# Newton's steps of two inverse roots, column by column or over all columns at once

## The chip, the core and the metric

The kernel runs on one core of a Trainium2 chip. A core has five engines that work side by side, each through its own list of instructions in order: TensorE (PE in the profile, with its weight loads as PEld), VectorE (DVE), ScalarE (ACT), GpSimd (POOL) and SyncE (SP), which here only issues transfers. The engines wait for one another by semaphores. The metric is the time of one execution on the device in microseconds (us). Lower is better.

## The reference, cut to what matters

The reference is one layer of a sequence encoder over 1024 tokens of 1024 channels. It normalises x, projects it, runs two mixers (a state-space scan, S5, and Hyena, which convolves with long filters), merges them and projects again. Two inverse square roots matter here.

The first belongs to Hyena's filters. Each of 2048 filters (2 orders, 1024 channels) has its own two-sided response k of 2048 steps, scaled to unit length:

```
k = k * lax.rsqrt(jnp.sum(k * k, axis=0, keepdims=True) + HY_EPS)
```

The second belongs to the RMSNorm of x, one number for each of 1024 tokens:

```
y = xf * lax.rsqrt(jnp.mean(xf * xf, axis=-1, keepdims=True) + RMS_EPS)
```

## The kernel before, in words

The first 260 us build the filters' spectra. The work is cut into eight units of 256 filters (order o, quarter cq). A unit has two parts. `filter_time` runs over eight tiles of 128 time steps: PE multiplies a small network's output into the tile (`g`, L333 and L334), ACT makes the decay (`e`, L336), DVE multiplies both (`e`, L338, one input from PSUM), ACT squares (`sq`, L342), DVE or POOL forms sums and differences (`so`, `ss`, `sd`, L349 and L350), ACT and DVE split those of the odd tiles in two parts (`sh`, `sl`, L109 and L113), and POOL adds up the squares (`acc`, L357, two SBUF inputs of 128x512). `filter_freq` is the cosine and sine transform of the unit before: PE multiplies (`po` L404, `pe` L414), DVE joins the halves (`ke` L425 and L426, `ko` L429 and L430).

Between them stands `filter_norm`: PE sums the squares over the partitions (`q`, L371), DVE adds the epsilon (`qs`, L375), calls `rsqrt` on a tile of 128x2, and forms from its result a correction that PE transposes (L381, L383) and DVE adds to one row of the sums (`ss`, L386). So `rsqrt` is called eight times with two columns (result `nrm`). `conv_weights` later reads all of `nrm` (L569 to L572).

In the same stretch `norm_in` prepares x piece by piece between the tiles of the units: four loads, sixteen squares on ACT, then on DVE the sum (`ssq`, L460, L462) and one call of `rsqrt` with eight columns (result `rs`), then ACT scales x by `rs` (`xr`, L468), PE transposes it (`xt`, L475), and ACT and DVE split it (`xh` L479, `xl` L480). The sums over x are taken while the second unit runs and the root while the third does.

`rsqrt` (L115) starts from a bit trick (L119), scales v by -0.5 (L121), and takes three Newton steps y = y (1.5 + v y y). A step is written column by column: L125 forms z = (y v) y for one column, with v as a scalar per partition, and L126 forms y = (z + 1.5) y. With two columns that is 12 instructions, with eight columns 48, each on a tile of 128x1.

The order of each engine's list is set when the program is built, by a planner that simulates the timeline (`schedule_with_timeline_sim=True`) and picks among the instructions that are ready by priority. `filter_norm` has raised priority (L285). `issue_after` (L288, L291) ties the other parts to steps of `filter_time`. The planner may put other instructions between the steps of one `rsqrt`.

After the units come the projections (`pps`, L556), S5, the Hyena convolutions and the output, mostly on PE.

Of the kernel before, what the change touches and what calls it, by code (L numbers as in the profile page):

```python
# [12 lines left out]
ALU = mybir.AluOpType  # L13
# [87 lines left out]
class Trunk:  # L101
# [13 lines left out]
    def rsqrt(self, pool, out, v, n):  # L115

        V = self.nc.vector
        h = pool.tile([128, n], F, name="rsq_h", tag="rsq_h")
        V.tensor_scalar(out=out.bitcast(I32), in0=v.bitcast(I32), scalar1=-0.5, scalar2=float(0x5F3759DF),  # L119
                        op0=ALU.mult, op1=ALU.add)  # L120
        V.tensor_scalar(out=v, in0=v, scalar1=-0.5, scalar2=None, op0=ALU.mult)  # L121
        for _ in range(3):
            for c in range(n):
                y, z = out[:, c:c + 1], h[:, c:c + 1]
                V.scalar_tensor_tensor(out=z, in0=y, scalar=v[:, c:c + 1], in1=y, op0=ALU.mult, op1=ALU.mult)  # L125
                V.scalar_tensor_tensor(out=y, in0=z, scalar=1.5, in1=y, op0=ALU.add, op1=ALU.mult)  # L126

    def reduce_2pi(self, out, x, k):
        nc = self.nc
# [1410 lines left out]
```

## Time and profile before

| | us |
|---|---|
| median of 3 runs | 1416.13 (1413.56 to 1418.54) |
| the profiled execution | 1413.96 |
| its span in the trace | 1412.2 |
| PE busy | 1346.7 (95%) |
| DVE busy | 1014.1 (72%), 1934 instructions |
| ACT busy | 515.1 (36%) |
| POOL busy | 416.6 (29%) |
| chain that ended last | PE 72%, DVE 18% of the span |

Times in a profile are microseconds from the start of the span. Busy time is summed over the instructions of an engine. A busy PE is not PE at its peak, since its records are pipelined. PEclk is the clock that was granted to TensorE as a share of 2.4 GHz. The chain that ended last is followed back from the last instruction: at each step to what released it, or to the instruction before it on its engine.

### The profile page before, as it was taken

To read this page: it belongs to the slowest core of one execution; us is meant where nothing else is said; L and a number is where in the kernel's file an instruction comes from. 1 tells how busy PE (TensorE), PEld (TensorE's weight loads), DVE (VectorE), ACT (ScalarE), POOL (GpSimd) and SP (SyncE) were. 2 spreads that over 40 slices of the span, in tenths; PEclk is the share of its full clock that TensorE was granted. 3 is DMA by queue.
4 is the path that set the end of the run, shared out by engine and by line. 5 is a ranking of instruction groups with operands and counts; after the bars stand their busy time and mean duration, and the time that the engine had idled before them with its cause. 6 is when DMAs were issued, how large, how long until landed. Compare 5 with 4: busy or idle time off the path is not lost.

```text
span 1412.2 us, 19536 instructions
## 1 busy us (share of the span) xinstructions
PE 1346.7 (95%) x7219; PEld 1135.9 (80%) x7219; DVE 1014.1 (72%) x1934; ACT 515.1 (36%) x737; POOL 416.6 (29%) x343
## 2 busy tenths in 40 slices
PE   5888899999999999999999997999999999999997
PEld 3777798888888887788788885998888889878886
DVE  7999997699599887414479997663899836843632
ACT  5576664222332333333322222443222234422422
POOL 3766675000000000223112213743013223322322
PEclk9999999999999999999999998999999999999999
DMA  8222224865695554566985588769888988755431
GB/s 278 94 78 75 77 100 146 200 173 137 164 301 132 124 124 103 134 173 155 307 244 173 172 241 264 216 179 315 258 268 268 292 247 245 220 161 134 139 112 64
DMA packets 188556, 257.24 MB, mean 182 GB/s; under 512 B 23069, under 2 KB 144153, under 8 KB 185724
## 3 DMA queue, kind: packets, MB, share of 16 engines
q1 hardware_dynamic: 148492, 151.32, 34.0%
q0 software_dynamic: 12608, 43.79, 15.6%
q10 hardware_dynamic: 27360, 60.88, 12.0%
q8 instruction: 57, 0.93, 0.3%
q14 instruction: 39, 0.32, 0.1%
HBM read 147.49 MB, written 76.82 MB: 159 GB/s over the span
## 4 chain that ended last, share of the span: by engine, by line
PE 72%; DVE 18%; DMA 5%; issue 3%; ACT 1%; POOL 1%; SPq 0%; ACTq 0%; DVEq 0%; POOLq 0%
PE pps L556 43%; PE ops L1441 6%; PE iv L643 5%; PE po L404 4%; PE fwo L695 3%; DMA zc<-c_zc_lo_d 2%; PE pe L414 2%; PE pps L536 2%; DVE rsq_h L125 2%; DVE e L338 1%; PE fwe L695 1%; DMA d_y<-x 1%; DVE st L1274 1%; PE zt L680 1%; DVE st L1272 1%
## 5 line engine op out<-in xcount | busy, mean ns | idle before, releaser
L512 POOL DMA_DIRECT2D wlo<-wraw x76 | 66.3, 872 | 673.3 <-ACT wlo L511 530.2
L556 PE MATMUL pps<-xh,whi 128*128 128x512 f32 x848 | 214.2, 400 | 3.2 <-DVE cv L581 3.2
L556 PE MATMUL pps<-xl,whi 128*128 128x512 f32 x848 | 212.3, 397 | 0.0
L556 PE MATMUL pps<-xh,wlo 128*128 128x512 f32 x848 | 210.2, 396 | 0.0
L556 PEld LDWEIGHTS pps<-xh,whi 128*128 128x128 f32 x848 | 158.0, 189 | 39.5 <-ACT wlo L511 3.6
L556 PEld LDWEIGHTS pps<-xh,wlo 128*128 128x128 f32 x848 | 157.9, 188 | 36.8
L556 PEld LDWEIGHTS pps<-xl,whi 128*128 128x128 f32 x848 | 157.3, 188 | 36.3 <-issue 0.2
L510 ACT CAST whi<-wraw 128x1024 fp32r<-128x1024 f32 (+1 forms) x76 | 74.7, 982 | 285.7 <-PE pps L556 254.9
L404 PE MATMUL po<-sh,fo 128*128 128x256 f32 x512 | 101.1, 292 | 6.0 <-DVE sh L111 5.1
L643 PE MATMUL iv<-ic,y 128*128 128x256 f32 (+1 forms) x752 | 97.2, 287 | 5.5 <-POOL y L113 3.1
L643 PEld LDWEIGHTS iv<-ic,y 128*128 128x128 f32 x752 | 95.4, 194 | 8.1 <-POOL y L113 4.0
L404 PEld LDWEIGHTS po<-sh,fo 128*128 128x128 f32 x512 | 84.0, 197 | 8.3 <-DVE sh L111 6.1
L357 POOL TENSOR_TENSOR acc<-acc,sq 128x512 f32<-128x512 f32 x56 | 75.9, 1356 | 24.5 <-ACT sq L342 23.0
L511 ACT ACTIVATE wlo<-whi 128x1024 fp32r<-128x1024 f32 (+1 forms) x76 | 74.9, 985 | 20.7 <-PE pps L556 20.6
L113 DVE TENSOR_TENSOR y<-yraw,y 128x512 fp32r<-128x512 f32 x60 | 55.0, 938 | 28.2 <-ACT y L109 28.2
L404 PE MATMUL po<-sl,fo 128*128 128x256 f32 x256 | 74.2, 290 | 1.0 <-DVE sl L113 1.0
L579 DVE SCALAR_TENSOR_TENSOR cv<-pps,cw,cv 128x1023 f32<-128x1023 f32 x24 | 30.7, 1281 | 59.5 <-ACT cv L578 59.5
L109 ACT CAST y<-yraw 128x512 fp32r<-128x512 f32 x64 | 39.0, 619 | 55.9 <-DMA yraw<-d_y 27.4
L404 PEld LDWEIGHTS po<-sl,fo 128*128 128x128 f32 x256 | 50.4, 197 | 2.2 <-DVE sl L113 1.3
L578 ACT ACTIVATE cv<-pps,cb,cw 128x1024 f32<-128x1024 f32 x24 | 29.0, 1208 | 62.1 <-PE pps L556 43.9
L333 PE MATMUL g<-w3h,ha 128*128 128x512 f32 x64 | 33.3, 520 | 18.6 <-DVE e L338 17.6
L695 PE MATMUL fwo<-z,zc 128*128 128x256 f32 x384 | 49.9, 283 | 0.0
(447 smaller groups left out, 2788.7 us busy)
## 6 DMA issues: line engine op xcount, KB each, us to landing
wlo<-wraw POOLq DMA_DIRECT2D x64, 512.0 KB, 5.7
wraw<-w_in SPq DMA_DIRECT2D x56, 512.0 KB, 5.2
kspec<-ko SPq DMA_DIRECT2D x32, 512.0 KB, 3.6
kt<-kspec SPq DMA_DIRECT2D x32, 512.0 KB, 5.1
yraw<-d_y SPq DMA_DIRECT2D x64, 256.0 KB, 5.3
d_y<-x ACTq DMA_DIRECT2D x28, 512.0 KB, 5.5
d_m<-cv ACTq DMA_DIRECT2D x16, 512.0 KB, 2.6
d_z<-z ACTq DMA_DIRECT2D x8, 1024.0 KB, 5.5
```

The costliest lines, as they stand in the source:

```text
L109: nc.scalar.copy(out=hi, in_=src)
L113: e.tensor_tensor(out=lo, in0=src, in1=hi, op=ALU.subtract)
L333: nc.tensor.matmul(out=ps, lhsT=ha[:, tsl], rhs=w3h, start=True, stop=False)
L357: nc.gpsimd.tensor_tensor(out=acc, in0=acc, in1=sq, op=ALU.add)
L404: nc.tensor.matmul(out=po[:, part], lhsT=fo[a][:, 12 * (jj % 2) + b], rhs=sd[4 + i][d][:, part], start=n == 0 and part == 0, stop=n == 11 ...
L510: nc.scalar.copy(out=hi, in_=raw)
L511: nc.scalar.activation(out=lo, in_=hi, func=AF.Copy, scale=-1.0)
L512: nc.gpsimd.dma_start(out=lo, in_=raw, accum_op=ALU.add)
L556: self.summed = nc.tensor.matmul(out=ps[:, hf * 512:hf * 512 + 512], lhsT=w[:, kc], rhs=part(x, kc, hf), start=a == 0 and p == 0 and kc == ...
L643: self.rotated = nc.tensor.matmul(out=dst, lhsT=lhsT, rhs=self.ic[b, j][:, cols], start=first, stop=last)
L695: nc.tensor.matmul(out=out, lhsT=zc[a][:, b], rhs=z[:, :, d, zi], start=start and n == 0, stop=stop and n == 3 * len(prods) - 1)
L1441: nc.tensor.matmul(out=pss[cs.start][:, 0:cs.stop - cs.start], lhsT=m[:, kc, ts], rhs=w[kc][:, cs], start=kc == 0 and p == 0, stop=kc == 7 ...
```

## The change

Each Newton step is now three instructions over the whole tile, whatever the number of columns: h = y y, h = h v, y = (h + 1.5) y. A call has nine instructions in its steps, on 128x2 in `filter_norm` and on 128x8 in `norm_in`. The bit trick and the scaling ahead of them stay.

```diff
         for _ in range(3):
-            for c in range(n):
-                y, z = out[:, c:c + 1], h[:, c:c + 1]
-                V.scalar_tensor_tensor(out=z, in0=y, scalar=v[:, c:c + 1], in1=y, op0=ALU.mult, op1=ALU.mult)
-                V.scalar_tensor_tensor(out=y, in0=z, scalar=1.5, in1=y, op0=ALU.add, op1=ALU.mult)
+            V.tensor_tensor(out=h, in0=out, in1=out, op=ALU.mult)
+            V.tensor_tensor(out=h, in0=h, in1=v, op=ALU.mult)
+            V.scalar_tensor_tensor(out=out, in0=h, scalar=1.5, in1=out, op0=ALU.add, op1=ALU.mult)
```

## Rows read from the trace of the kernel before

**Rows 1.** The page, chain that ended last, shares of the span by engine.

```profile
PE 72%; DVE 18%; DMA 5%; issue 3%; ACT 1%; POOL 1%; SPq 0%; ACTq 0%; DVEq 0%; POOLq 0%
```

**Rows 2.** Busy time by stretch, one filter unit each: stretch, length, busy, PEclk, DMA.

```profile
45.40:70.50 25.10, 21.47 (x119) 18.23 (x120) 24.65 (x50) 15.91 (x27) 19.30 (x19) 0.93 0.31 111
70.50:97.80 27.30, 23.80 (x147) 20.80 (x147) 25.62 (x49) 23.13 (x56) 18.90 (x20) 0.97 0.25 86
97.80:132.90 35.10, 29.41 (x171) 25.70 (x171) 34.33 (x104) 17.84 (x32) 19.79 (x21) 0.87 0.24 88
132.90:160.70 27.80, 25.77 (x160) 23.03 (x160) 27.25 (x52) 19.77 (x36) 18.48 (x20) 0.94 0.23 80
160.70:185.90 25.20, 22.20 (x144) 19.76 (x144) 24.06 (x51) 16.83 (x30) 20.78 (x20) 1.00 0.21 72
185.90:213.10 27.20, 27.14 (x184) 24.76 (x184) 27.10 (x55) 19.09 (x32) 20.45 (x23) 1.00 0.25 96
213.10:237.50 24.40, 23.01 (x152) 20.59 (x151) 22.87 (x47) 10.71 (x19) 17.50 (x18) 1.00 0.22 87
237.50:260.00 22.50, 22.50 (x148) 20.76 (x148) 10.51 (x47) 5.28 (x6) 1.78 (x2) 1.00 0.90 236
```

**Rows 3.** The same view, finer, inside the third unit.

```profile
115.00:122.00 7.00, 6.98 (x22) 5.67 (x23) 7.00 (x21) 6.43 (x12) 4.07 (x5) 0.62 0.19 71
```

**Rows 4.** The chain in order of time, third unit: start, us on the chain, what.

```profile
112.54 0.60 DVE rsq_h L125
113.14 1.23 DVE rs L126 x2
114.37 0.61 DVE e L338
...
116.24 3.41 PE pe L414 x8
...
120.08 1.90 PE pe L414 x8
```

**Rows 5.** Groups of DVE instructions, 40 to 250 us: count, busy, mean ns of one.

```profile
L125 DVE SCALAR_TENSOR_TENSOR rsq_h<-nrm,qs 128x1 f32<-128x1 f32 x48 | 21.9, 490 | 0.2
...
L126 DVE SCALAR_TENSOR_TENSOR nrm<-rsq_h,nrm 128x1 f32<-128x1 f32 x48 | 10.2, 233 | 0.0
...
L125 DVE SCALAR_TENSOR_TENSOR rsq_h<-rs,ssq 128x1 f32<-128x1 f32 x24 | 8.2, 358 | 0.0
...
L126 DVE SCALAR_TENSOR_TENSOR rs<-rsq_h,rs 128x1 f32<-128x1 f32 x24 | 4.4, 196 | 0.0
```

**Rows 6.** DVE in order of time, the eighth call: start, us, what, idle before.

```profile
237.87 0.17 DVE L121 TENSOR_SCALAR qs<-qs 128x2 f32<-128x2 f32 x1
238.07 0.35 DVE L125 SCALAR_TENSOR_TENSOR rsq_h<-nrm,qs 128x1 f32<-128x1 f32 x2
238.34 0.28 DVE L126 SCALAR_TENSOR_TENSOR nrm<-rsq_h,nrm 128x1 f32<-128x1 f32 x2
...
239.45 0.34 DVE L381 SCALAR_TENSOR_TENSOR qs<-qs,nrm,par 128x1 f32<-128x1 f32 x2
239.71 0.16 DVE L569 TENSOR_SCALAR nrm_s<-nrm 128x16 f32<-128x16 f32 x1
239.91 0.35 DVE L571 TENSOR_TENSOR cw<-par,nrm_s 128x16 f32<-128x16 f32 x3
240.17 0.17 DVE L572 TENSOR_TENSOR cb<-par,nrm_s 128x16 f32<-128x16 f32 x1
242.84 0.41 DVE L386 SCALAR_TENSOR_TENSOR ss<-q,ss 1x256 f32<-1x256 f32 x1 [2.50 <-PE q L383]
```

**Rows 7.** DVE and POOL in order of time, in the fourth call.

```profile
134.09 1.44 DVE L125 SCALAR_TENSOR_TENSOR rsq_h<-nrm,qs 128x1 f32<-128x1 f32 x2
135.46 0.68 DVE L338 SCALAR_TENSOR_TENSOR e<-e,g 128x512 f32<-128x512 f32 x1
136.05 0.92 DVE L126 SCALAR_TENSOR_TENSOR nrm<-rsq_h,nrm 128x1 f32<-128x1 f32 x2
...
134.22 2.67 POOL L357 TENSOR_TENSOR acc<-acc,sq 128x512 f32<-128x512 f32 x2 [0.48 <-POOL so L350]
```

**Rows 8.** Waits in the third unit, 98 to 133 us: total us, times, longest.

```profile
ACT xr L468 <- DVE rs L126: 2.7, 1, 2.7
```

## The prediction

> **What bounds the kernel now.** I read the chain of waits first: PE holds 72% of it and DVE 18% [rows 1], so an edit on DVE can only pay in the stretch where DVE is on the chain. The view of busy time by stretch, cut at the start of each of the filters' normalisations, shows that stretch [rows 2]. In the units from 45 to 237 us DVE is busy for 22.9 to 34.3 us of 24.4 to 35.1, between 94 and 100%, while PE leaves 0.1 to 5.7 us of a unit idle. From 237.5 us on it is the other way: PE fills 22.50 of 22.50 and DVE 10.5. So the first seven units are bound by DVE with PE close behind, and what follows by PE. The reader is to see one unit that stands out. The third lasts 35.10 us. The six others last 25.10, 27.30, 27.80, 25.20, 27.20 and 24.40, on average 26.2. The third is 8.9 us longer, and has 104 instructions on DVE where the others have 47 to 55. It is the unit that holds the eight-column call.
>
> The chain in order of time says the same from inside: up to 114.4 us it runs along DVE and through Newton's steps, then it passes to PE [rows 4]. PE is idle for 5.7 us of this unit [rows 2], and right behind that its clock is down: 0.62 granted between 115 and 122 us, a mix of the levels 2.4 and 1.2 GHz [rows 3]. Eight matmuls of L414 stand on the chain for 3.41 us at 116.24 and for 1.90 at 120.08 [rows 4].
>
> **The change part by part.** I price three things: the eight-column call, what PE's clock gives back, and the eight two-column calls.
>
> The eight-column call. Its 48 instructions are busy for 8.2 + 4.4 = 12.6 us [rows 5]. Their durations overlap: two L125 start at 238.07, take 0.35 and would end at 238.42, but the next starts at 238.34 [rows 6], 0.08 earlier. So 48 x 0.08 = 3.8 us are counted twice, and 8.8 us of DVE's time go. That this equals the 8.9 us by which the unit is too long supports it. In their place come nine instructions, each of which reads what the one before wrote. The nearest rows for such a pair are L121 at 237.87 with L125 at 238.07, and L569 at 239.71 with L571 at 239.91: 0.20 us from start to start in both [rows 6]. Width costs little: L571 on 128x16 starts three times in 240.17 - 239.91 = 0.26 us, 0.087 each [rows 6]. Nine steps are 9 x 0.20 = 1.8 us, with a lower bound of 9 x 0.087 = 0.8 if other instructions lie between them.
>
> To that come stops by POOL. Two L125 that normally take 0.35 took 1.44 while POOL's L357 ran, and two L126 took 0.92; L338, which has one input from PSUM, took 0.68 beside the same POOL instructions [rows 7]. Unstopped, a step's instruction has (239.45 - 238.07) / 12 = 0.115 us [rows 6], so the 48 would need 5.5 us, and 8.8 - 5.5 = 3.3 us were stops. The new call lies in a shorter stretch and meets fewer of POOL's instructions; between 0 and 3.3 us I take 0.8. Net: 1.8 + 0.8 - 8.8 = -6.2 us.
>
> What is late next: POOL's instructions are still there and can stop another one on DVE that reads two tiles of SBUF. That gives back between 0 and the 3.3 us; I take 1.5, a little under half, since the ones that read PSUM pass [rows 7]. ACT, which waited 2.7 us for `rs` [rows 8], scales x earlier, and the transposes and splits behind it move forward; they are moved, not added, and nothing is queued past a transfer.
>
> PE's clock. If DVE no longer holds PE up ahead of 115 us, PE has less idle time there and the eight matmuls should take 1.90 in place of 3.41: -1.5 us. The bounds are 0 and, if all of the unit ran at the full level, (1 - 0.87) x 35.1 = 4.6 us [rows 2].
>
> The two-column calls. Each goes from 12 instructions to nine. Unstopped they took 1.38 us (238.07 to 239.45), because the two columns alternate and an instruction need not wait for the one ahead of it [rows 6]. Nine dependent ones take 9 x 0.20 = 1.80: +0.42 a call. Where the planner lays other work between them, as L338 at 135.46 [rows 7], the wait is hidden and they take down to 9 x 0.087 = 0.78: -0.60. Eight calls lie between -4.8 and +3.4 us. Dependence is the nearer row for a chain of nine, so I weight it double: (2 x 0.42 - 0.60) / 3 = 0.08, or +0.1 a call and +0.8 in all. The stops in these calls: (21.9 + 10.2) - 96 x 0.08 = 24.4 us of room [rows 5], less 8 x 1.38 = 11.0, leaves 13.4 us, about 1.9 for each of the seven calls that POOL meets. They are set by how long POOL's burst lasts, two L357 in 2.67 us [rows 7], not by how many instructions wait, so I take no change. Below it could be a quarter less (three of 12 instructions fewer), -3.4; above, one more L357 of 1.33 us in each of seven calls, +9.3.
>
> The eighth call costs nothing either way: behind it L386 waits 2.50 us for PE [rows 6], and PE is full. That cover would have to shrink below 0.4 us to matter.
>
> One rule speaks on that term. The row shows that neighbours which don't depend on each other start 0.115 us apart, dependent ones 0.20 [rows 6]. The Trainium skill, "VectorE: DVE Perf Modes", section "The DRAIN you can't avoid", says instead that the next instruction starts only once the pipeline has emptied and that a semaphore between them adds nothing; by that, nine instructions for 12 would cost three quarters, 8 x 1.38 x (-0.25) = -2.8 us, and the whole would come to -9.0. The rows contradict it here: the overlap of 0.08 is there only between independent ones.
>
> The sum: -6.2 + 1.5 - 1.5 + 0.8 = -5.4 us. All of it lies in units where DVE is 94 to 100% busy, and PE behind them has no start that is fixed otherwise, so I count it in full at the end. The profiled execution took 1413.96 us, 1.8 more than its span of 1412.2, and lies 2.2 below the median of 1416.13. From the profile that is 1408.6, against the median 1410.7 us.
>
> **The rivals.** First, most is given back. All 3.3 us of stops fall on DVE's other instructions in the third unit and every two-column call pays its 0.42: -6.2 + 3.3 - 1.5 + 3.4 = -1.0, 1415.1 us. For it: POOL is busy for 17.5 to 20.8 us in each of the seven units (the fifth busy time) [rows 2], so there is always one to be met. Against: DVE's instructions that read PSUM passed POOL's unstopped, as L338 did [rows 7].
>
> Second, the number of instructions decides. Other work fills every gap, -4.8 for the eight calls, and no stops move: -6.2 - 1.5 - 4.8 = -12.5, 1403.6 us. For it: DVE has other work ready nearly always in units 1 to 7. Against: the eighth call, where nothing was ready, and PE, which is 99.8% busy in the sixth unit and would take over as the bound there.
>
> Third, slower. The nine instructions all read two tiles of SBUF and form one chain, so a POOL instruction that slips in ahead of any of them holds the rest, and no second column is there to run meanwhile. If a call meets one more L357 in seven calls and pays 0.42 in eight, that is +9.3 + 3.4, against -6.2 + 1.5 - 1.5: +6.5, 1422.6 us. It decides from (6.2 + 4.25) / 8 = 1.3 us of extra time a call on. For it: two L126 behind the stopped L125 were stopped again [rows 7]. Against: POOL's bursts are two such instructions long and then wait for DVE. The Trainium skill, "SBUF — State Buffer", section "Who interferes with whom", has the port that both engines share as an exclusive lock; rows 7 agree, 1.44 us against 0.35.
>
> **How the numbers follow.** A measurement of this kernel can tell about 0.3%, 4.25 us, from no change. I give the forecast 0.55, of which 0.07 falls short of that bound; the first rival 0.22, the second 0.13, the third 0.10. So faster 0.48 + 0.13 = 0.61, the same 0.07 + 0.22 = 0.29, slower 0.10. The planner's whole list may also shift by a few microseconds behind the change, which no row prices. The range goes from 1402, a little beyond the second rival, to 1419, beyond the first and short of the third. The forecast's own range is 1405 to 1414.
>
> **What would show it.** In the profile after, `rsqrt` should have 81 instructions in its steps in place of 144, and a dependent pair should start 0.20 us apart. The third unit should last 27 to 29 us, its L414 should show no pair of 1.90 and 3.41, and the PEclk of its slices should be near that of its neighbours. The other units should stay within 1 us of their lengths. The prediction is wrong if the third unit shortens by under 4 us, if the others lengthen by more than a microsecond each, or if the saving is there at 260 us and gone at the end.

## The result: slower by 0.8%, and the profile after

The changed kernel took 1427.15 us (median of 4 runs, 1426.87 to 1428.43) beside 1417.34 for the kernel before on the same chip: a ratio of 1.0077, 95% interval 1.0062 to 1.0093. The forecast was 1410.7. The profiled execution took 1428.43 us with a span of 1426.6. In the four groups of experiments below the kernel before, timed beside them with 12 to 35 runs, had medians of 1416.6 to 1417.4 us; the ratios are to these.

The steps themselves did about what the prediction said. The groups of DVE's instructions in the changed kernel (its lines 123 to 125 are the three instructions of a step, its later lines stand one lower than before; columns as in [rows 5]) are these:

```profile
L124 DVE TENSOR_TENSOR rsq_h<-rsq_h,qs 128x2 f32<-128x2 f32 x24 | 10.2, 424 | 0.6
L123 DVE TENSOR_TENSOR rsq_h<-nrm 128x2 f32<-128x2 f32 x24 | 9.1, 379 | 0.4
L125 DVE SCALAR_TENSOR_TENSOR nrm<-rsq_h,nrm 128x2 f32<-128x2 f32 x24 | 7.6, 316 | 0.6
L124 DVE TENSOR_TENSOR rsq_h<-rsq_h,ssq 128x8 f32<-128x8 f32 x3 | 1.3, 428 | 0.0
L125 DVE SCALAR_TENSOR_TENSOR rs<-rsq_h,rs 128x8 f32<-128x8 f32 x3 | 1.0, 323 | 0.0
L123 DVE TENSOR_TENSOR rsq_h<-rs 128x8 f32<-128x8 f32 x3 | 0.5, 161 | 0.0
```

The eight-column call is down to 2.8 us of busy time from 12.6 [rows 5], the two-column calls to 26.9 from 32.1. Part of that is no gain, since the busy times of before overlap. From each row's start to the next's, less idle time, the eight-column call took 2.2 us in place of 9.5, and the seven two-column calls ahead of the eighth took 25.6 in place of 26.4. So DVE has some 8 us less of them, and yet the stretch is longer. The view of busy time by stretch for the changed kernel, cut at the start of each normalisation as in [rows 2], shows where:

```profile
46.40:72.00 25.60, 21.46 (x130) 18.20 (x131) 25.36 (x46) 15.73 (x27) 18.53 (x18) 1.00 0.32 106
72.00:99.30 27.30, 22.64 (x138) 19.28 (x137) 25.25 (x45) 23.06 (x55) 18.87 (x20) 0.99 0.24 86
99.30:130.50 31.20, 27.52 (x146) 23.84 (x145) 24.83 (x56) 17.21 (x31) 18.78 (x20) 0.79 0.23 84
130.50:163.20 32.70, 28.45 (x179) 25.45 (x178) 29.29 (x56) 20.48 (x36) 18.69 (x20) 0.95 0.23 85
163.20:191.10 27.90, 25.54 (x167) 22.59 (x167) 27.44 (x50) 19.51 (x34) 20.83 (x22) 1.00 0.19 75
191.10:218.30 27.20, 25.62 (x171) 22.80 (x170) 25.90 (x49) 17.04 (x29) 18.96 (x21) 1.00 0.22 85
218.30:248.50 30.20, 25.70 (x155) 22.55 (x154) 23.25 (x43) 11.43 (x20) 16.88 (x19) 0.94 0.18 70
248.50:271.00 22.50, 22.50 (x148) 20.70 (x147) 9.72 (x43) 4.69 (x5) 1.78 (x2) 1.00 0.91 236
```

The chain that ended last is followed back only to 214 us in this trace (its shares sum to 83%), so it serves for the units behind that point alone:

```profile
PE 65%; DVE 12%; DMA 5%; issue 1%; ACT 0%; SPq 0%; DVEq 0%; ACTq 0%
```

The third unit is 3.9 us shorter than in [rows 2], but the fourth is 4.9 longer, the fifth 2.7 and the seventh 5.8. DVE, which was 94 to 100% busy in every unit, is idle for 6.4 us of the third, 3.4 of the fourth and 7.0 of the seventh. Some work has moved from the third unit into the fourth (PE has 146 and 179 instructions there, and had 171 and 160). Over the seven units DVE has less work, 181.3 us in place of 185.9, but they last 202.1 us in place of 192.1. The engines wait for one another more.

The eighth call starts at 248.5 us where it started at 237.5, so 11.0 of the 14.4 us by which the two profiled spans differ are lost by then. The other 3.4 can't be put down to the order: behind that call, the kernel before took 1174.7 us in its profile and a kernel with the same lists 1176.8 (the changed kernel in the order of before, below).

The planner's lists are what differs. With Newton's instructions left out, the two kernels issue the same 10,153 instructions, of which 148 of DVE's, 494 of PE's, 90 of ACT's, 9 of POOL's and 11 of SyncE's stand at another place of their list. That counts places: an instruction that moves also shifts those that it passes. The last of them issue some 280 us after the start in the kernel before and 291 us in the changed one; from there on the lists are the same.

### The profile page after: what moved, and what is told of

Its sections match the earlier page's. It is cut to its first block, busy times and chain, and to the rows that moved or that the text cites. A ratio compares the mean times of both kernels' runs of the same rounds, so it can differ in the third digit from the quotient of the medians.

```text
span 1426.6 us, 19467 instructions
## 1 busy us (share of the span) xinstructions
PE 1353.5 (95%) x7219; PEld 1140.3 (80%) x7219; DVE 1009.2 (71%) x1871; ACT 515.2 (36%) x737; POOL 406.3 (28%) x343
## 4 chain that ended last, share of the span: by engine, by line
PE 65%; DVE 12%; DMA 5%; issue 1%; ACT 0%; SPq 0%; DVEq 0%; ACTq 0%
PE pps L555 41%; PE ops L1440 6%; PE iv L642 5%; PE fwo L694 3%; DMA zc<-c_zc_lo_d 2%; DMA d_y<-x 2%; PE pps L535 2%; PE fwe L694 1%; PE po L403 1%; DVE st L1273 1%; PE zt L679 1%; DVE st L1271 1%; PE pe L413 1%; DVE y L113 1%; PE s5ps L1223 1%
```

## The experiments

Each kernel was timed in five rounds beside the kernel before on the same chip.

### Parts of the change, each laid out by the planner

The first two take one kind of call each over all columns (shown for the two-column calls; the other has n == 8), the third leaves all of Newton's steps out, the fourth moves x's first scaling.

```diff
-        for _ in range(3):
+        for _ in range(3 if n == 2 else 0):
             V.tensor_tensor(out=h, in0=out, in1=out, op=ALU.mult)
...
+        for c in [c for _ in range(0 if n == 2 else 3) for c in range(n)]:
...
```

> Only the eight two-column calls take their steps over all columns; the eight-column call stays column by column. Theory A (price: the chain of nine dependent instructions is stopped by POOL more often than the old twelve): the loss is here, 1422 to 1430 us, and Newton's steps of the nrm calls take more of DVE than the 26.4 us of before. Theory B (early rs: the x work that hangs on rs moves forward and lands badly): within 3 us of before, 1413 to 1420. Theory C (any change of the list makes the planner lay out the whole stretch anew, for better or worse): a shift of up to 12 us either way, with DVE busy for no longer but idle for longer.

> Only the eight-column call is taken over all columns; the two-column calls stay as before. Theory A: the saving of the prediction without its costs, 1408 to 1412 us. Theory B: all of the loss is here, 1424 to 1430 us, with the third unit only some 4 us shorter and DVE idle in it for 5 us or more. Theory C: anything from 1405 to 1430, and the sum of the shifts of this and of the two-column kernel is not the shift of the whole change (+10).

```diff
-        for _ in range(3):
-            V.tensor_tensor(out=h, in0=out, in1=out, op=ALU.mult)
-            V.tensor_tensor(out=h, in0=h, in1=v, op=ALU.mult)
-            V.scalar_tensor_tensor(out=out, in0=h, scalar=1.5, in1=out, op0=ALU.add, op1=ALU.mult)
```

> Newton's steps are left out altogether (both roots keep only their first estimate), so some 36 us of DVE's time in the stretch go and nothing is added. Theory A: well faster, 1395 to 1403 us, since the price is in the steps. Theory B: the early rs hurts just as much, so clearly less than that: 1408 to 1420. Theory C: the layout decides; time not ordered by how much work the steps are, DVE idle in the seven units clearly above the 6 us of before.

```diff
         self.xl = {}
+        yield
         for hf, ch in parts:
...
                 nc.scalar.activation(out=r[:, i], in_=r[:, i], func=AF.Copy, scale=rs[:, 4 * hf + i:4 * hf + i + 1])
-            yield
+            if (hf, ch) != parts[0]:
+                yield
```

> The changed kernel, with the scaling of x's first part by rs put off by one slot of the plan (three tiles of the unit), to join its first transposes; every instruction is the same. Theory B: a good part of the loss comes back, 1415 to 1421 us, and the third unit's wait of DVE for sh (2.8 us) is gone. Theory A: no change from the changed kernel, 1426 to 1429. Theory C: a shift of several us either way, that the third unit alone does not explain.

| kernel | median, us | ratio to before, 95% interval |
|---|---|---|
| two columns only | 1424.38 | 1.0051 (1.0035 to 1.0068) |
| eight columns only | 1417.83 | 1.0008 (0.9995 to 1.0020) |
| no steps | 1411.47 | 0.9956 (0.9939 to 0.9972) |
| scaling later | 1414.14 | 0.9979 (0.9967 to 0.9991) |

Theory A, price, failed on three of these. The eight-column call alone gained nothing where it should have gained 4 us or more, and leaving out 36 us of DVE's time gained 6. The two-column kernel's time lies in the range of theory A, but its seven calls took 23.9 us of DVE from start to start, not more than the 26.4 of before. Theory B, the early `rs`, failed on the two-column kernel, which has a late `rs` and loses 7 us all the same, and on the eight-column kernel, which should have had all of the loss. Moving the scaling by one slot brought back 13 us with the same instructions, but not where I had put it. The third unit's wait for `sh`, which was to be gone, fell from 2.8 to 1.6 us, as two of the four scalings still stood ahead of `sh`, and that unit lasted 31.4 us; the fourth fell from 32.7 to 26.2 and the seventh from 30.2 to 27.5. That left theory C, the lists as a whole, though its own sign is not clear: the shifts of the two parts, 7.2 and 1.1 us, fall short of the whole change's 10.9 by no more than their intervals allow.

### The same instructions in either order

To part the instructions from their order, each engine's list can be held. An edge that sets only the order of issue is laid from every instruction to the next one of its engine, in the order taken from the other kernel (`ORDER`, packed). Newton's steps stand where that kernel has its own: `plain` are the instructions without the steps, `steps` those by call and number.

```diff
+def in_order(tc, nc):
...
+    for line in json.loads(zlib.decompress(base64.b85decode(ORDER))):
+        queue = [steps[n] if n >= 20000 else plain[n] for n in line]
+        for before, i in zip(queue, queue[1:]):
+            tc.add_manual_dep(i, before.name, info, reason="order")
...
         Trunk(tc, ins, outs).run()
+        in_order(tc, nc)
```

> The changed kernel's instructions, with the list of every engine held in the order of the kernel before (nine steps stand where the first column's steps stood; everything else is at its place of before). Theory order (the loss is the planner's new order): faster than before, by the room that the eight-column call gives up less what is waited for otherwise, 1407 to 1413 us. Theory price (chains of nine cost more than the columns): as slow as the changed kernel or nearly, 1423 to 1429.

> The kernel before's instructions, with the list of every engine held in the order of the changed kernel (a step's columns stand together where its three instructions stood). Theory order: at least as slow as the changed kernel, 1426 to 1436 us, as the eight-column call costs its room again. Theory price: about the kernel before, 1413 to 1420.

> Only the eight-column call over all columns, in the order of the kernel before. Theory order: 1408 to 1413 us; beside the run of the whole change in this order it gives the price of the two-column calls by itself (my term: +0.8, between -4.8 and +12.7). Theory price: this one is clearly faster than the whole change in the same order, by 5 us or more.

> No Newton step at all (left out), in the order of the kernel before: what the steps of both roots cost in that order. They fill 36 us of DVE. If every one of them is on the path, 1380 to 1385 us; if PE takes over as the bound at once, 1405 to 1412. Theory order expects between, 1393 to 1405, and in any case less than the 1411.5 that the planner's own order gave without the steps.

| instructions | in the order of before | in the order of the changed kernel | as the planner lays them out |
|---|---|---|---|
| before | 1 | 1.0098 (1.0080 to 1.0117), 1432.29 us | 1 |
| changed | 0.9943 (0.9923 to 0.9963), 1409.13 us | 1.0077 (1.0062 to 1.0093) | the same |
| eight columns only | 0.9944 (0.9923 to 0.9965), 1408.74 us | | 1.0008 |
| no steps | 0.9872 (0.9852 to 0.9892), 1399.55 us | | 0.9956 |

This settles that the order makes the loss. In the order of before, the change is 0.57% faster, 8.1 us of 1417. In its own order the same instructions are 1.35% slower than that (1.0077 / 0.9943), 19 us. And the order alone, with not one instruction changed, makes the kernel before 1% slower. The changed kernel in the order of before beats both kernels. The gain of 0.57% belongs to that order: in the other one the changed instructions are 0.2% faster than the old ones (1.0077 and 1.0098), and the intervals overlap.

A kernel held in its own order was not run. But the edges can't be the cause by themselves, since they made one kernel faster and the other slower. In the traces, PE's, DVE's and POOL's lists of both held kernels are those of the kernel that the order came from, with as many semaphore instructions on each engine.

With its own instructions in the order of the changed kernel, the kernel before has long units in the same places. Its fourth and seventh, which last 27.8 and 24.4 us in [rows 2], are these:

```profile
135.20:167.80 32.60, 28.35 (x179) 25.38 (x178) 29.54 (x58) 20.64 (x36) 18.70 (x20) 0.95 0.24 89
223.00:252.80 29.80, 25.36 (x155) 22.42 (x154) 23.39 (x47) 11.34 (x20) 16.80 (x19) 0.94 0.18 71
```

The busy time by stretch of the changed kernel in the order of before is what the prediction had described:

```profile
46.30:71.10 24.80, 20.40 (x124) 17.55 (x125) 24.48 (x47) 15.83 (x27) 18.72 (x18) 1.00 0.31 111
71.10:98.50 27.40, 23.52 (x148) 20.14 (x147) 25.48 (x46) 23.13 (x55) 18.90 (x20) 1.00 0.24 87
98.50:127.00 28.50, 26.01 (x175) 23.37 (x174) 28.25 (x62) 18.66 (x34) 19.16 (x20) 1.00 0.28 102
127.00:153.50 26.50, 24.27 (x157) 21.16 (x156) 26.29 (x49) 19.98 (x34) 19.22 (x20) 1.00 0.24 89
...
178.60:205.90 27.30, 27.23 (x185) 24.70 (x184) 26.89 (x52) 19.12 (x32) 20.42 (x23) 1.00 0.25 96
205.90:230.50 24.60, 22.90 (x151) 20.47 (x150) 22.73 (x43) 10.73 (x19) 17.47 (x18) 1.00 0.22 87
```

The third unit lasts 28.5 us, DVE is busy for 28.25 of them, and the granted clock is 1.00 in all of these units. The fourth is 1.3 us shorter than in [rows 2]; the others are within 0.3 us of their lengths.

### Which list, and where in it

> The changed kernel, with PE's list alone held in the order of the kernel before; the planner lays out the other engines' lists around it. If the loss is in PE's list (transposes and the norm's small matmuls put ahead of work that was ready), 1407 to 1413 us. If it is in DVE's and ACT's lists, 1418 to 1428.

> The changed kernel, with DVE's list alone held in the order of the kernel before. If the loss is in DVE's list (long multiplications put behind the chain of nine steps), 1407 to 1413 us; if it is in PE's, 1418 to 1428. Both this one and the one with PE's list held fast would mean that either list carries the other along.

Here `in_order` got one list alone. With PE's list held the changed kernel took 1416.69 us (0.9998, 0.9988 to 1.0009), with DVE's 1411.44 (0.9962, 0.9949 to 0.9976). Against the changed kernel's own 1.0077 that is 0.8% and 1.15% back, of the 1.35% that the whole order is worth. DVE's list brings back most, as its expectation had it; PE's fell between its two ranges. The two shares add up to more than the whole, so they overlap: the planner lays the other lists out around the one that is held.

As a control, the kernel before got one instruction of 0.16 us more, so that the planner laid it out anew: in one kernel in the third call of `filter_norm` (shown), in the other ahead of the eight-column steps, on v.

```diff
+        if col == 4:
+            nc.vector.tensor_scalar(out=qs, in0=qs, scalar1=1.0, scalar2=None, op0=ALU.mult)
```

> The kernel before, with one instruction of 0.16 us more on DVE (the third unit's sums times 1.0, ahead of its root); the planner's order changes in 37 rows of DVE's list, 10 of ACT's and 4 of PE's. If any new order costs as the changed kernel's does: 1421 us or more, far beyond 0.16 us. If the order of before is nothing special, 1415 to 1419.

> The kernel before, with one instruction of 0.16 us more on DVE ahead of the eight-column root; the order changes in 26 rows of DVE's list, 10 of ACT's and 7 of PE's. If any new order costs: 1421 us or more; if not, 1415 to 1419.

They took 1416.39 us (0.9998, 0.9986 to 1.0010) and 1418.07 (1.0008, 0.9995 to 1.0021). So not every new order costs time. These were small changes of the lists, and cost nothing that can be measured.

The last three hold DVE's list in the order of before in one stretch each.

> The changed kernel, with DVE's list held in the order of before in the seventh unit alone (from ahead of its root to ahead of the eighth's); the rest is the planner's. If the seventh unit's own order makes its 5.8 us (30.2 against 24.4), that unit falls to 24 to 26 us and the time to 1420 to 1423. If it only pays for what came before, it stays at 29 us or more and the time at 1425 to 1429.

> The changed kernel, with DVE's list held in the order of before up to the fourth call, so through the eight-column call; the planner's own behind it. If the early scaling of x in the third unit is what the loss hangs on, the third unit falls to 28 to 29 us, the fourth from 32.7 to below 28, and the time to 1412 to 1420 with the seventh unit still long. If the two-column calls' order behind it is enough for the loss, the time stays above 1422.

> The changed kernel, with DVE's list held in the order of before from the fourth call to the seventh. If the loss sits in the fourth and fifth units' own order, they fall by 6 us or more together, to 1418 to 1421; if it follows from the third unit's early scaling of x, the fourth stays at 30 us or more and the time at 1424 or more.

| DVE's list held | median, us | ratio | units 3, 4 and 7, us |
|---|---|---|---|
| nowhere (changed kernel) | 1427.15 | 1.0077 | 31.2, 32.7, 30.2 |
| seventh unit alone | 1419.74 | 1.0021 (1.0007 to 1.0035) | 28.6, 32.8, 25.2 |
| up to the fourth call | 1421.81 | 1.0033 (1.0017 to 1.0048) | 30.2, 29.9, 30.1 |
| fourth to seventh call | 1420.22 | 1.0014 (0.9996 to 1.0032) | 30.5, 30.1, 27.7 |

The seventh unit's own order makes its length: held there, 30.2 us become 25.2. The rest lies in the third to fifth units, which are 2.7, 6.2 and 2.8 us longer than in the order of before, and does not come apart so neatly. Holding the third took 1.0 us off it and 2.8 off the fourth; holding the fourth to the sixth took 2.6 us off the fourth and 2.5 off the seventh, which was not held. Neither brings the fourth back to the 26.5 us of the order of before, and in neither run did one of the two expected outcomes come out whole.

### What the order does in the seventh unit

DVE in order of time in the changed kernel's seventh unit, around the end of the call's first step (start, us, what, idle before):

```profile
222.06 0.67 DVE L337 SCALAR_TENSOR_TENSOR e<-e,g 128x512 f32<-128x512 f32 x1
222.65 0.24 DVE L125 SCALAR_TENSOR_TENSOR nrm<-rsq_h,nrm 128x2 f32<-128x2 f32 x1
222.89 0.27 DVE L339 MEMSET e<- 1x256 f32 x1
223.09 0.49 DVE L123 TENSOR_TENSOR rsq_h<-nrm 128x2 f32<-128x2 f32 x1
223.62 1.20 DVE L124 TENSOR_TENSOR rsq_h<-rsq_h,qs 128x2 f32<-128x2 f32 x1
224.85 0.66 DVE L125 SCALAR_TENSOR_TENSOR nrm<-rsq_h,nrm 128x2 f32<-128x2 f32 x1
225.55 0.65 DVE L123 TENSOR_TENSOR rsq_h<-nrm 128x2 f32<-128x2 f32 x1
226.23 1.19 DVE L124 TENSOR_TENSOR rsq_h<-rsq_h,qs 128x2 f32<-128x2 f32 x1
227.46 0.16 DVE L125 SCALAR_TENSOR_TENSOR nrm<-rsq_h,nrm 128x2 f32<-128x2 f32 x1
...
230.69 0.68 DVE L337 SCALAR_TENSOR_TENSOR e<-e,g 128x512 f32<-128x512 f32 x1
```

The same place in the changed kernel in the order of before (its line numbers are 22 or 23 higher):

```profile
211.50 1.20 DVE L147 SCALAR_TENSOR_TENSOR nrm<-rsq_h,nrm 128x2 f32<-128x2 f32 x1
212.74 0.16 DVE L145 TENSOR_TENSOR rsq_h<-nrm 128x2 f32<-128x2 f32 x1
212.93 0.16 DVE L146 TENSOR_TENSOR rsq_h<-rsq_h,qs 128x2 f32<-128x2 f32 x1
213.13 0.16 DVE L147 SCALAR_TENSOR_TENSOR nrm<-rsq_h,nrm 128x2 f32<-128x2 f32 x1
213.32 0.35 DVE L403 SCALAR_TENSOR_TENSOR qs<-qs,nrm,par 128x1 f32<-128x1 f32 x2
213.59 0.68 DVE L360 SCALAR_TENSOR_TENSOR e<-e,g 128x512 f32<-128x512 f32 x1
```

The reader is to see where the next long multiplication `e` stands. In the order of before it starts 0.3 us behind the end of the steps (213.29 to 213.59). In the new order it comes at 230.69, 3.1 us behind their end, after two splits, two sums and a piece of x. One more `e`, at 222.06, stands inside the first step instead. Of the six instructions of the second and third step behind it, five were stopped while POOL worked (0.49 to 1.20 us where 0.16 is the plain length; POOL is busy from 222.1 to 227.4 us without a break). PE, in order of time, is then held up by three things in a row:

```profile
227.93 0.45 PE L382 MATMUL q<-ident,qs 128*128 128x128 f32 x2 [1.30 <-DVE qs L380]
228.13 0.47 PE L333 MATMUL g<-w3l,ha 128*128 128x512 f32 x1
230.12 0.66 PE L474 MATMUL xt<-ident,xr 128*128 128x128 f32 x4 [1.51 <-DVE xl L479]
231.43 0.53 PE L332 MATMUL g<-w3h,ha 128*128 128x512 f32 x1 [0.66 <-DVE e L337]
231.77 0.61 PE L333 MATMUL g<-w3l,ha 128*128 128x512 f32 x1
232.18 1.91 PE L413 MATMUL pe<-sd,fe 128*128 128x256 f32 x4
```

Its granted clock falls behind that, from 1.00 to 0.73 (columns as in [rows 2]):

```profile
220.00:228.00 8.00, 6.70 (x45) 5.91 (x43) 7.79 (x18) 3.17 (x6) 6.55 (x8) 1.00 0.07 27
232.00:238.00 6.00, 4.96 (x18) 3.83 (x18) 3.27 (x6) 3.03 (x6) 6.00 (x8) 0.73 0.00 0
```

In its list the second half of `g` (L333) stands behind `q`, and `q` waits for the call. In the order of before `q` stood ahead of both halves, and waited 0.65 us. Four matmuls of the same line then took 1.02 us in place of 1.91, at a granted clock of 1.00 from 212 to 220 us:

```profile
213.60 0.45 PE L405 MATMUL q<-ident,qs 128*128 128x128 f32 x2 [0.65 <-DVE qs L403]
213.81 0.48 PE L355 MATMUL g<-w3h,ha 128*128 128x512 f32 x1
...
214.35 1.02 PE L436 MATMUL pe<-sd,fe 128*128 128x256 f32 x4
```

The third unit has a wait of another sort. ACT scales four pieces of x in a row as soon as `rs` is there, and the split `sh` that DVE needs stands behind them (ACT, then DVE, in order of time in the changed kernel):

```profile
109.97 2.56 ACT L467 ACTIVATE xr<-xr,rs 128x512 f32<-128x512 f32 x4 [0.87 <-DVE rs L125]
112.43 0.60 ACT L109 CAST sh<-so 128x512 fp32r<-128x512 f32 x1
```

```profile
113.06 0.69 DVE L113 TENSOR_TENSOR sl<-so,sh 128x512 fp32r<-128x512 f32 x1 [2.81 <-ACT sh L109]
```

In the kernel before `rs` came late and column by column, and the first four scalings lay apart (at 114.40, 116.16 for two, and 120.17 us). This wait alone does not make the third unit's length: with the scaling put off it was 1.2 us shorter, and the unit was 31.4 us long, against 31.2.

## Why the prediction was wrong, point by point

**What bounds the kernel** held. Leaving all the steps out in the order of before gave 18 us, half of the 36 that they fill on DVE (26.4 in the first seven two-column calls and 9.5, from each row's start to the next's, less idle time). PE takes over on the way: the sixth unit then is 26.1 us with PE busy for all of them.

**The eight-column call** held in the order of before. There the third unit goes from 35.1 to 28.5 us, -6.6, against -6.2 for the call, -1.5 for the clock and +1.5 for later stops. With this call alone changed, the third unit lasts 28.8 us and the time falls by 7.9 us (0.9944 of 1417); as the planner lays out the same instructions, that unit lasts 34.0 us.

**PE's clock** came back in that order: 1.00 in the third unit in place of 0.87, and four matmuls of L414, which took 1.91 us at 116.03 and at 117.74, take 1.02 to 1.03 from 111 to 115 us. In the changed kernel's own order it went the other way, to 0.79, although PE is idle for 3.7 us of that unit, less than the 5.7 of before.

**The two-column calls** held in the price of a chain. In the eighth call, where nothing lies between, the nine took 250.74 - 248.99 = 1.75 us, 0.195 from start to start, where I had 1.80:

```profile
248.99 0.15 DVE L123 TENSOR_TENSOR rsq_h<-nrm 128x2 f32<-128x2 f32 x1
...
250.74 0.35 DVE L380 SCALAR_TENSOR_TENSOR qs<-qs,nrm,par 128x1 f32<-128x1 f32 x2
```

All eight calls together cost nothing that the runs can tell: 0.9943 with them and 0.9944 without. I had +0.8 us, and with intervals of some 3 us to either side the times can't tell that from the -2.8 us that I took from the Trainium skill, "VectorE: DVE Perf Modes", section "The DRAIN you can't avoid". I used only half of that section: it lets the next instruction start when the pipeline has emptied, but adds that one that isn't held starts earlier. So it has room for the 0.115 us between alternating instructions, the rows don't contradict it as I wrote, and counting instructions does not follow from it. What decides here is the spacing in the trace: 0.195 us in a dependent chain against 0.115.

**The third rival**, slower, named 1422.6 us, the nearest figure, but for a reason that the runs contradict. It wanted the nine-step chains to meet more of POOL's stops. From start to start, the seven calls ahead of the eighth took 25.6 us in the changed kernel, 27.3 in the same kernel in the order of before, which is 1.35% faster, and 26.4 in the kernel before. Even in the seventh unit POOL stopped five of the call's nine instructions in the new order and four in the order of before.

**The step that failed** is the sentence that "the planner's whole list may also shift by a few microseconds behind the change, which no row prices". I gave it no place in the sum and no width in the range. It measured +19 us, more than twice the gain of 8.1 and of the other sign. I had also written of the work behind `rs` that "they are moved, not added", and priced the move at nothing. Moved work was the point: x's scaling and transposes, the second half of `g` and the order of `e` and the steps. My reading, which no run tests, is that DVE and PE were both nearly full in every unit, so that there was little slack in which a worse order could hide. The prediction's own signs said the same: the third unit shortened by under 4 us, and three others lengthened by more than one.

**What stays open.** Why the planner's simulated timeline ranks the instructions as it does is not shown by any run. Why the clock was low in the changed kernel's third unit is open too. In the third to fifth units, the loss is shown to come from the order, but not from one place in it. Of the other layouts by the planner, eight columns only lost 9 us and no steps 12 us against the same instructions in the order of before, and the two controls lost nothing; so how a layout falls out can't be told from the size of the edit by these runs.

## What to carry to other kernels

Where a planner sets the order of the lists, an edit is two edits: the instructions and the order. Before pricing the first, ask what hangs on the result that now comes earlier, and put a term for the second into the range; here it was 19 us beside a gain of 8. And when a sound saving comes out slower, hold the old order and time the new instructions in it: that run and its mirror image told the two apart, and none of the kernels that keep Newton's steps was clearly faster than it.

## What the runs showed that was not expected

One list gave two lengths. In the kernel with DVE's list held in the seventh unit alone, the lists of all engines are those of the changed kernel up to the seventh unit. Its third unit, in the same view as above, is 2.6 us shorter, at another granted clock (28.6 us at 0.94 against 31.2 at 0.79):

```profile
98.80:127.40 28.60, 24.01 (x143) 20.39 (x143) 24.70 (x57) 17.12 (x31) 18.85 (x20) 0.94 0.24 85
...
215.30:240.50 25.20, 23.41 (x151) 20.70 (x150) 22.59 (x43) 11.22 (x20) 18.05 (x19) 1.00 0.24 91
```

So one list can give lengths of a unit that differ by 2 to 3 us between two profiles. Whether that varies from one execution to the next or goes with the kernel is not shown: the four timed runs of the changed kernel lie within 1.6 us, and the median with the seventh unit held is 7.4 us lower, of which that unit's own 5.0 are only a part. Unit lengths of single profiles are to be read with that in mind. The timed ratios above don't rest on them.
